# A recurrent scan on one core: the DMA queue in written order, stores one place later, solver pieces behind the state update, evictions on ScalarE, new pools

## The chip, the cores and the metric

The kernel runs on one core of a Trainium2 chip. A core has five engines that run their own instruction streams side by side: TensorE (PE, matrix multiplication; its weight loads are listed as PEld), VectorE (DVE), ScalarE (ACT), GpSimd (POOL) and SyncE (SP), whose queue issues the DMA transfers of this kernel. The metric is the device time of one execution in microseconds (us).

## The reference

One layer of a diffusion backbone on 128 context tokens and 1024 latent tokens of width 1024: a gated feed-forward, a mixer and a second gated feed-forward, each with a residual and a layer norm. The mixer projects its input once, and then runs an RWKV-7 branch and a pooling branch, gates both by channel, adds them and projects again. All of it is float32. Cut to the part that the change touches:

```
def _rwkv7_step(S, inp):                  # one token, both directions, 16 heads of 64
    r, w, k, v, kk, a = inp
    sa = jnp.einsum('dbhvk,dbhk->dbhv', S, kk)
    S = S * w[..., None, :] - sa[..., :, None] * (kk * a)[..., None, :] + v[..., :, None] * k[..., None, :]
    return S, jnp.einsum('dbhvk,dbhk->dbhv', S, r)
...
    s_final, y = lax.scan(_rwkv7_step, s0.astype(f32), xs)
    y = _from_scan(y)                     # forward plus reversed backward
    mu = jnp.mean(y, -1, keepdims=True)
    var = jnp.mean(jnp.square(y - mu), -1, keepdims=True)
    y = ((y - mu) * lax.rsqrt(var + GN_EPS)).reshape(b, t, D_A) * p['lnx_g'] + p['lnx_b']
    bonus = jnp.sum(r_h * k_h * p['r_k'], -1, keepdims=True) * v_h
    y = (y + bonus.reshape(b, t, D_A)) * g
    y_a = y.astype(h.dtype) @ p['w_o_rwkv']
    ...                                   # pooling branch: windows of 2, 4, 8, 16 tokens, w_pool, pool_scale
    y_b = u @ p['w_o_pool']
    gate_a = jax.nn.sigmoid(gate_logits[..., :D_MODEL])
    gate_b = jax.nn.sigmoid(gate_logits[..., D_MODEL:])
    return (gate_a * y_a + gate_b * y_b) @ p['w_out'], s_final
```

The latent scans start from given states (one for each direction); the context scans start from zero, and their last states are an output.

## The kernel before, in words

Tokens lie in NB = 3 blocks of 384. A float32 product is made of three matmuls: both operands are split into a high and a low part (`split`; for weights ACT makes `wh`, POOL or DVE `wl`), and high·high, high·low and low·high are added in PSUM. The stages follow each other: the first feed-forward, the mixer's input projection, a stage "m2", the scan (pools "s1" and "gn"), and then the rest of the mixer and the second feed-forward ("stage e" here).

The scan takes tokens in chunks of 64, both directions (d = 0, 1) at once, eight heads at a time: 18 chunks for each half of the heads, 36 steps. One step, `main(s)`, does the following. `xy` (L1042) multiplies the chunk's operands `ak` by the states `Sc`, and L1048 adds the part of the tokens before; the result is copied to `Xs`, d = 0 by ACT and d = 1 by DVE (L1052). `us` (L1058) multiplies `Xs` by the inverse `W` of a triangular matrix; it goes to `vu`, again by ACT and by DVE (L1062, L1064). `sp` (L1071) multiplies `vu` by the transposed keys `KBT`, and DVE adds it to the states and decays them (L1072, L1073). L1077 makes the output, ACT copies it to `yt` (L1081), and every second step stores it.

Between these parts lie three slots. Slot 0 stands behind the `Xs` copies, slot 1 behind `vu`, slot 2 behind the output. `slot_work(s, k)` puts into a slot a piece of a solver and one piece of each group norm under way, `fill(k)` some matmuls of `filler`. Slot 0 also has `pre(s+3)` (loads of `ak`, L998) and `pre_lm` (L1011 on PE, L1013 on DVE: the masked products `LM` for the next step); slot 2 is preceded by `load` (v of a unit of two steps, L985), `pre_kb` (transposes of keys, L1019) and `pre_lm`.

- `filler` is the gate and pooling branch: 900 matmuls of 128x384 outputs. `Halves` brings its weights in halves of 512 columns (load L139, ACT split L148, POOL split L149). `proj(n)` makes a gate from `hg` (the stored mixer input of blocks 1 and 2, loaded at L897), the four pool gemms (`pw`) take a pooled input `uf` (L923) each, and `back(n)` multiplies a gate by its branch (`gt`, L918) and stores it (`gab`, L919). AHEAD = 60 of them run before step 0. The others are spread over the slots in the ratio SPREAD = 6 : 9 : 10.
- `solve(i)` inverts the triangular 32x32 blocks of two units (four steps). It is a generator; `slot_work` takes a piece in each slot over four steps. It loads `Gq` and `Gt` (L758, eight DMAs), POOL transposes the half of d = 1 (L762), 31 pairs on DVE (L766, L768) work out both inverses, four pairs a slot, the result goes to memory and comes back in other layouts (`Wb`, `Dx`, `Nt`), and matmuls `ph` join the blocks to 64x64 inverses. Solvers 0 and 1 begin in m2, the other seven run in the scan.
- `group_norm(hb, tt)` is a generator in nine pieces for 128 tokens: loads and sums of `y`, the variance on DVE (L1122, L1123), a power on POOL (L1124), a product (L1125), four transposes on PE (L1132), scaling on ACT, the bonus on POOL (L1138) and the store `yn` (L1139). `drive` moves each running one by a piece; behind the last step a loop drives what is left, three pieces a round.

In the scan the order on PE, DVE, ACT and POOL is the order in which the code is written; the DMA queue of SP, and all engines outside of the scan, are ordered by a scheduler.

Of the kernel before, what the change touches and what calls it, by code (L numbers as in the profile page):

```python
# [2 lines left out]

# [17 lines left out]
AHEAD = 60  # L21
SPREAD = (6, 9, 10)
PWGAP = 4
# [37 lines left out]
def tile_step(ctx: ExitStack, tc: tile.TileContext, I: dict, O: dict):  # L61
# [68 lines left out]
    class Halves:  # L130
# [11 lines left out]
        def get(self, i, look=2):  # L142
            while len(self.got) < min(len(self.units), i + 1 + look):
                self.fetch(len(self.got) + 1)
                r = self.raws[len(self.got)]
                h = self.pool.tile([P, self.HW], F32R, name="wh", tag="wh", bufs=4)
                l = self.pool.tile([P, self.HW], F32R, name="wl", tag="wl", bufs=4)
                A.copy(h, r)  # L148
                G.tensor_tensor(l, r, h.bitcast(F32), ALU.subtract)  # L149
# [446 lines left out]
    with pool("mp", 4, psum=True) as psum, pool("ma", 2, psum=True) as paux, \  # L596
# [6 lines left out]
        with pool("m1") as pl:  # L603
# [11 lines left out]
            for p in range(NP):  # L615
# [26 lines left out]
                for b in range(NB):  # L642
# [79 lines left out]
                    S.dma_start(nd_d[1][p // 4][b][:, p % 4].rearrange("s c e t -> s (c e) t"), Qs[96:128, :, :, 0:32].rearrange("s c e t -> s (c e) t"))  # L722
# [24 lines left out]
        def solve(i):  # L747
            def t4(nm, tag_):
                return sv.tile([P, 32, 32], F32, name=nm, tag=tag_)
            Gq, Gt = t4("Gq", "gq"), t4("Gt", "pr")  # L750
            for k in range(2):
                u = 2 * i + k
                for d in range(2):
                    c0 = chunk0(u, d)
                    cb, cc, hb = c0 // 6, c0 % 6, u // 9
                    for hf in range(2):
                        p0 = d * 64 + hf * 32 + k * 16
                        S.dma_start((Gt if d else Gq)[p0:p0 + 16], qd_d[d][hb][cb][hf][:, cc:cc + 2].rearrange("a c e s t -> a (c e) (s t)"))  # L758
            Wd = t4("Wd", "wd")
            S.dma_start(Wd, I["id32"])  # L760
            yield
            G.tensor_copy(Gq[64:128], Gt[64:128].rearrange("p s t -> p t s"))  # L762
            pr = t4("pr", "pr")
            for k in range(31):
                o = pr[:, 0:k + 1, k + 1:32]
                V.tensor_tensor(o, Wd[:, 0:k + 1, k].unsqueeze(2).broadcast_to([P, k + 1, 31 - k]),  # L766
                                Gq[:, k, k + 1:32].unsqueeze(1).broadcast_to([P, k + 1, 31 - k]), ALU.mult)
                V.tensor_tensor(Wd[:, 0:k + 1, k + 1:32], Wd[:, 0:k + 1, k + 1:32], o, ALU.subtract)  # L768
                if k % 4 == 3:
                    yield  # L770
            ed = dram.tile([2, 2, 32, 32, 32], F32, name="ed", tag="ed", bufs=2)
            S.dma_start(ed.rearrange("d b n i t -> (d b n) i t"), Wd)
            yield
            W = Wb[i % 2]
            DT = Dx = t4("Dx", "dx")
            Mt = Nt = t4("Nt", "nt")
            for b in range(2):
                S.dma_start(W[32 * b:32 * b + 32, :, 32 * b:32 * b + 32], ed[0, b].rearrange("n i t -> i n t"))
                S.dma_start(Dx[64 + 32 * b:96 + 32 * b], ed[1, b].rearrange("n i t -> i n t"))
            for k in range(2):  # L780
                u = 2 * i + k
                for d in range(2):
                    c0 = chunk0(u, d)
                    S.dma_start(Nt[96 * d:96 * d + 32, k * 16:k * 16 + 16].rearrange("s (a n) t -> s a (n t)", a=4),
                                nd_d[d][u // 9][c0 // 6][:, :, c0 % 6:c0 % 6 + 2].rearrange("s a c e t -> s a (c e t)"))
            yield
            V.transpose(DT[0:32], W[0:32, :, 0:32])
            for b in range(2):
                r = slice(64 + 32 * b, 96 + 32 * b)
                V.transpose(W[r, :, 32 * b:32 * b + 32], Dx[r])  # L790
            yield

            def ph(jobs, k):
# [6 lines left out]
            for k in range(2):  # L800
                ks = slice(16 * k, 16 * k + 16)
                pm = ph(lambda n: ((slice(32, 64), Nt[0:32, n, :], DT[0:32, n, :]), (slice(64, 96), Nt[96:128, n, :], Dx[96:128, n, :])), k)
                A.copy(Mt[32:64, ks], pm[32:64])
                A.copy(Mt[64:96, ks], pm[64:96])
                yield
                pm = ph(lambda n: ((slice(0, 32), Mt[32:64, n, :], W[32:64, n, 32:64]), (slice(96, 128), Mt[64:96, n, :], W[64:96, n, 0:32])), k)
                A.mul(W[0:32, ks, 32:64], pm[0:32], -1.0)
                A.mul(W[96:128, ks, 0:32], pm[96:128], -1.0)
                yield

        CHAIN, TAILS, PPS = 11, 4, [paux, "aux"]
# [4 lines left out]
        for t in vus[0] + vus[1]:  # L816
            G.memset(t, 0.0)
        with pool("m2") as pl:
            sol0, sol1 = solve(0), solve(1)
            for _ in range(CHAIN + TAILS):  # L820
                next(sol0)
            for _ in range(CHAIN):
                next(sol1)
# [58 lines left out]

    def filler(psG):
# [7 lines left out]
        for b in range(NB):  # L891
            sl = slice(b * BN, (b + 1) * BN)
            hh = hs[0]
            if b:
                hh = [hpA.tile([P, KT, BN], F32R, name="hg", tag="hb") for k in range(2)]
                for k in range(2):
                    S.dma_start(hh[k].bitcast(F32), h2_d[b][k])  # L897
# [6 lines left out]
            def proj(n):  # L904
                ps = psG.tile([P, 512], F32, name="pm", tag="mm")
                for hf in range(2):
                    w = nextw(1 if n == 0 and hf else 2)
# [5 lines left out]
            def back(b, u2, gts, n):  # L913
# [5 lines left out]
                S.dma_start(gab_d[n][b][:, 1, :], gt)  # L919
# [8 lines left out]
            first = proj(0)  # L928
# [18 lines left out]
            for n in range(1, 8):  # L947
# [7 lines left out]
    with pool("s1") as pl, pool("gn") as gn, pool("spa", 2, psum=True) as psA, pool("spx", 1, psum=True) as psX, \  # L955
# [22 lines left out]
        def load(u):  # L978
            hb, q, cs = steps[2 * u]
            c = ctxs[u]  # L980
            for d in range(2):
                c0 = cs[d] // 2 * 2
                vh = slice(64, 128) if d == 0 else slice(0, 64)
                r0 = (c0 % 6) * 64
                S.dma_start(vus[d][u % 2][vh].rearrange("p k h v -> p k (h v)"),  # L985
                            vt_d[c0 // 6][r0:r0 + 128, 512 * hb:512 * hb + 512].rearrange("(k t) c -> t k c", k=2))
            c["W"] = Wb[u // 2 % 2][:, u % 2 * 16:u % 2 * 16 + 16].rearrange("p (a k e) t -> p a k e t", a=4, k=2)

        def pre(s):
            u = s // 2  # L990
            if s % 2 == 0:
                ctxs[u] = {"ak": {}, "LM": {}, "KBT": {}}
            hb, q, cs = steps[s]
            c = ctxs[u]
            c["ak"][s] = []
            for d in range(2):
                ak = pl.tile([P, 4, 256], F32, name=f"ak{d}", tag=f"ak{d}", bufs=3)
                S.dma_start(ak, ak_d[d][cs[d] // 6][cs[d] % 6, :, 4 * hb:4 * hb + 4])  # L998
                c["ak"][s].append(ak)
            c["LM"][s], c["KBT"][s] = {}, {}  # L1000

        def pre_lm(s, d):
            c = ctxs[s // 2]
            ak = c["ak"][s][d]
# [10 lines left out]
        def pre_kb(s, d):  # L1015
            c = ctxs[s // 2]
            pt = psM.tile([P, 4, P], F32, name="pt", tag="m")
            for i in range(4):
                PE.transpose(pt[:, i, :], c["ak"][s][d][:, i, 128:256], ident)  # L1019
# [3 lines left out]
        def main(s):  # L1023
# [6 lines left out]
            ak = c["ak"].pop(s)  # L1030
# [19 lines left out]
            for d in range(2):  # L1050
                x0, x1 = XR[d]
                (V.tensor_copy if d else A.copy)(eh(Xs[x0:x1]), xy[x0:x1, :, d])  # L1052
# [6 lines left out]
            for d in range(2):  # L1059
                x0, x1 = XR[d]  # L1060
                if d:
                    V.tensor_scalar(vu[d][x0:x1], us[x0:x1], -1.0, None, ALU.mult)  # L1062
                else:
                    A.mul(vu[d][x0:x1], us[x0:x1], -1.0)  # L1064
# [331 lines left out]
```

## Time and profile before

| | |
|---|---|
| median of three runs | 3551.59 us (3547.95 to 3558.2) |
| profiled execution, its own time | 3556.99 us |
| its span | 3555.2 us |
| mean granted TensorE clock | 0.943 |
| PE busy | 3263.3 us, 92% of the span, 25742 matmuls |
| DVE, ACT, POOL busy | 2053.9, 1104.4, 1315.4 us |
| scan, first step's first matmul to the last | 1707 to 2430 us |
| stage m2 | 1526 to 1652 us |

The profile is one execution. A row of a group names line, engine, operation, output and inputs with shapes and count, then busy time in us, the mean of one in ns, and the engine's idle time before them with what ended most of it. A row of the timeline gives start, length, engine and line, and in brackets the idle time before. The granted clock is a share of TensorE's full speed. The span does not hold 1.8 us of the execution's own time.

### The profile page before, as it was taken

The page shows a single profiled execution, that of the slowest core. Times are in us where ns is not written, and L with a number is a line of the kernel's source. Part 1 is how long each engine was busy: PE and PEld are TensorE (multiplying, and loading weights), DVE is VectorE, ACT ScalarE, POOL GpSimd, SP SyncE. Part 2 cuts the span into 40 slices and gives each one's busy share as a digit, 9 for nine tenths or more (in the row PEclk, how much of TensorE's full clock was granted, in tenths as well). Part 3 has the DMA queues.
Part 4 walks back from the last instruction along what each step waited for, and adds up shares of the span by engine and source line. Part 5 has one row for each costly group of instructions (what it writes and reads, how often), then busy time and mean ns, then how long its engine had stood idle before and what let it go on. Part 6 is the DMA issues. An engine that isn't in the chain of part 4 may idle for free.

```text
span 3555.2 us, 62714 instructions
## 1 busy us (share of the span) xinstructions
PE 3263.3 (92%) x25742; PEld 3094.7 (87%) x25742; DVE 2053.9 (58%) x3381; ACT 1104.4 (31%) x1898; POOL 1315.4 (37%) x1035
## 2 busy tenths in 40 slices
PE   7999999999999999787888777995999999999997
PEld 7999999998988877586777676885999999999996
DVE  6888532357467787855566676644576233222466
ACT  4111111125444444422333333333345111111133
POOL 5111111136466676643222343136774111111144
PEclk9999999999999999798898888997999999999998
DMA  6344211124645455465355555645652111111133
GB/s 232 127 144 133 75 48 37 54 89 143 217 146 160 155 160 155 144 199 169 117 151 188 148 155 174 170 123 172 223 177 66 40 45 37 48 48 36 48 124 108
DMA packets 309694, 442.74 MB, mean 125 GB/s; under 512 B 115360, under 2 KB 211104, under 8 KB 307872
## 3 DMA queue, kind: packets, MB, share of 16 engines
q1 hardware_dynamic: 309408, 438.74, 39.0%
q8 instruction: 202, 3.31, 0.4%
q14 instruction: 84, 0.69, 0.1%
HBM read 316.01 MB, written 101.25 MB: 117 GB/s over the span
## 4 chain that ended last, share of the span: by engine, by line
PE 58%; DVE 17%; DMA 8%; issue 7%; POOL 6%; ACT 3%; SPq 1%; DVEq 0%; POOLq 0%; ACTq 0%
PE pg L158 8%; PE pg L159 8%; PE pg L157 8%; PE po L158 5%; PE po L157 5%; PE po L159 4%; PE pm L158 2%; PE pm L157 2%; PE pm L159 2%; DVE Wd L768 2%; DVE pr L766 2%; DMA fm<-in_w_mod 2%; DVE wl L126 2%; PE xy L1042 2%; DVE fm L402 2%
## 5 line engine op out<-in xcount | busy, mean ns | idle before, releaser
L124 ACT CAST wh<-wr 128x1024 fp32r<-128x1024 f32 x270 | 280.3, 1048 | 818.2 <-PE po L158 432.9
L126 POOL TENSOR_TENSOR wl<-wr,wh 128x1024 fp32r<-128x1024 f32 x117 | 290.1, 2480 | 509.8 <-ACT wh L124 485.6
L294 POOL TENSOR_TENSOR gl<-sg,gh 128x384 fp32r<-128x384 f32 x132 | 159.0, 1205 | 780.6 <-ACT gh L293 780.5
L126 DVE TENSOR_TENSOR wl<-wr,wh 128x1024 fp32r<-128x1024 f32 x153 | 224.6, 1472 | 242.7 <-ACT wh L124 241.5
L157 PE MATMUL po<-gh,wh 128*128 128x384 f32 x1056 | 357.0, 338 | 7.4 <-ACT gh L293 4.3
L158 PE MATMUL pg<-h1l,wh 128*128 128x384 f32 x1056 | 356.6, 338 | 5.7 <-POOL h1l L166 5.7
L158 PE MATMUL po<-gl,wh 128*128 128x384 f32 x1056 | 357.7, 339 | 2.0 <-POOL gl L294 2.0
L157 PE MATMUL pg<-h1h,wh 128*128 128x384 f32 x1056 | 357.6, 339 | 0.0
L159 PE MATMUL po<-gh,wl 128*128 128x384 f32 x1056 | 355.8, 337 | 0.0
L159 PE MATMUL pg<-h1h,wl 128*128 128x384 f32 x1056 | 355.6, 337 | 0.0
L157 PE MATMUL pg<-h3h,wh 128*128 128x384 f32 x1056 | 353.7, 336 | 0.0
L159 PE MATMUL pg<-h3h,wl 128*128 128x384 f32 x1056 | 353.4, 335 | 0.0
L158 PE MATMUL pg<-h3l,wh 128*128 128x384 f32 x1056 | 353.2, 335 | 0.0
L291 DVE TENSOR_TENSOR sg<-sg,pg 128x384 f32<-128x384 f32 x132 | 74.2, 562 | 459.9 <-PE pg L159 453.9
L157 PE MATMUL pm<-h2h,wh 128*128 128x384 f32 x936 | 326.1, 348 | 3.7 <-ACT pads L441 3.7
L159 PE MATMUL pm<-h2h,wl 128*128 128x384 f32 x936 | 326.1, 348 | 0.0
L158 PE MATMUL pm<-h2l,wh 128*128 128x384 f32 x936 | 325.8, 348 | 0.0
L311 DVE SCALAR_TENSOR_TENSOR ac<-po,modh,ac 128x384 f32<-128x384 f32 (+1 forms) x352 | 173.0, 515 | 96.5 <-PE po L159 96.5
L149 POOL TENSOR_TENSOR wl<-wr,wh 128x512 fp32r<-128x512 f32 x75 | 96.5, 1292 | 321.9 <-ACT wh L148 264.2
L402 DVE SCALAR_TENSOR_TENSOR fm<-fm 128x512 f32<-128x512 f32 x224 | 182.3, 814 | 52.0 <-DMA fm<-in_w_mod 49.0
L157 PEld LDWEIGHTS po<-gh,wh 128*128 128x128 f32 x1056 | 199.1, 189 | 10.5 <-ACT gh L293 4.9
L158 PEld LDWEIGHTS pg<-h1l,wh 128*128 128x128 f32 x1056 | 200.5, 190 | 8.2 <-POOL h1l L166 7.7
(286 smaller groups left out, 7556.8 us busy)
## 6 DMA issues: line engine op xcount, KB each, us to landing
wr<-in_ffn_in SPq DMA_DIRECT2D x120, 512.0 KB
ak<-ak SPq DMA_DIRECT2D x48, 768.0 KB
ak<-ak SPq DMA_DIRECT2D x72, 512.0 KB
wr<-in_ffn_out SPq DMA_DIRECT2D x60, 512.0 KB
fm<-in_w_mod SPq DMA_DIRECT2D x112, 256.0 KB
wr<-in_w_mix SPq DMA_DIRECT2D x39, 512.0 KB
sh<-pads SPq DMA_DIRECT2D x108, 130.0 KB
wr<-in_w_mix SPq DMA_DIRECT2D x48, 256.0 KB
```

The source lines that it names most:

```text
L124: A.copy(h[:, :w], r[:, :w])
L126: e.tensor_tensor(l[:, :w], r[:, :w], h[:, :w].bitcast(F32), ALU.subtract)
L149: G.tensor_tensor(l, r, h.bitcast(F32), ALU.subtract)
L157: PE.matmul(ps, wh, xh, start=first and k == 0, stop=False)
L158: PE.matmul(ps, wh, xl, start=False, stop=False)
L159: PE.matmul(ps, wl, xh, start=False, stop=last and k == n - 1)
L291: lastv[0] = V.tensor_tensor(sg, sg, pu[:, :BN], ALU.mult)
L294: G.tensor_tensor(gs[j, b][1][:, sl], sg, gs[j, b][0][:, sl].bitcast(F32), ALU.subtract)
L311: lastv[0] = V.scalar_tensor_tensor(accs[b][:, n, s0:s1], po[:, s0:s1], modh[:, gate_i // 4, n, g:g + 1], accs[b][:, n, s0:s1], ALU.mult, ...
L402: V.scalar_tensor_tensor(jk, w, 1.0, silc[:, s, hf * 512:hf * 512 + 512], ALU.mult, ALU.mult, accum_out=part[:, kt, s, hf:hf + 1])
L766: V.tensor_tensor(o, Wd[:, 0:k + 1, k].unsqueeze(2).broadcast_to([P, k + 1, 31 - k]), Gq[:, k, k + 1:32].unsqueeze(1).broadcast_to([P, k + ...
L768: V.tensor_tensor(Wd[:, 0:k + 1, k + 1:32], Wd[:, 0:k + 1, k + 1:32], o, ALU.subtract)
```

## The change

- The DMA queue of SP joins the engines whose order in the scan is the written one.
- Stores of `y`, `yn` and `gab` in the scan are put on a list (`later`) and issued at the start of the next slot (`flush`).
- `solve` becomes a class with numbered pieces. Its pairs stand 2 in slot 0, 1 in slot 1 and 5 in slot 2, which lies behind the state update. The half of d = 1 is stored transposed already, by exchanging the operands of the matmul that makes it, so that the POOL copy goes. The parts that bring the inverse back take other places.
- The copies to `Xs` and `vu` of d = 1 move from DVE to ACT.
- A new pool `akp` holds `ak`; the loads of steps 0 to 2 and v of units 0 and 1 stand in m2, ahead of its gate work.
- AHEAD goes. 120 gate matmuls (TAILF) are kept for the time behind the last step: eight behind each drive, two drives a round in place of three. 780 are spread over the steps in place of 840.
- PWGAP is 10 in place of 4, and the matmuls between the pool gemms come from `proj(0)` and `proj(1)`. The `hg` loads move behind `back(6)` and `back(7)`, ahead of their first use, in four halves.
- `Halves.get` fetches one half ahead in place of two.
- A group norm has two more empty calls, one behind the power and one behind the bonus load's.

```diff
-AHEAD = 60
+TAILF = 120
-PWGAP = 4
+PWGAP = 10
...
-            self.fetch(len(self.got) + 2)
+            self.fetch(len(self.got) + 1)
...
+                                x, y = (al, be) if d else (be, al)
+                                pqs[b] = PE.matmul(pq[e][d * 64:d * 64 + 64, cc, :], ak[es, cc, x:x + 64], ak[es, cc, y:y + 64], start=True, stop=True)
...
+            def at(self, n):
+                if n == 0:
+                    self.loads()
+                elif n == 1:
+                    self.init()
+                elif n < 12:
+                    self.pairs((2, 1, 5)[n % 3])
+                elif n == 12:
+                    self.out()
+                elif n == 14:
+                    self.back()
+                elif n == 16:
+                    self.t0()
+                elif n == 17:
+                    self.t1(0)
+                elif n == 18:
+                    self.ph1(0)
+                elif n == 19:
+                    self.ph2(0)
+                elif n == 20:
+                    self.t1(1)
+                    self.ph1(1)
+                elif n == 21:
+                    self.ph2(1)
...
+            for s_, cs_ in enumerate(((0, 1), (1, 0), (2, 17))):
+                load_ak(s_, cs_, 0)
+            load_v(0, 0, (0, 1))
+            load_v(1, 0, (2, 17))
             for n in range(EARLY):
...
+    def later(out, in_):
+        lates.append((out, in_))
+
+    def flush():
+        while lates:
+            S.dma_start(*lates.pop(0))
...
-                for k in range(2):
-                    S.dma_start(hh[k].bitcast(F32), h2_d[b][k])
...
-                S.dma_start(gab_d[n][b][:, 1, :], gt)
+                later(gab_d[n][b][:, 1, :], gt)
...
-            first = proj(0)
+            if b:
+                for ks in (slice(0, 4), slice(4, 8)):
+                    for k in range(2):
+                        S.dma_start(hh[k][:, ks].bitcast(F32), h2_d[b][k][:, ks])
+            first = chain(proj(0), proj(1))
...
-                (V.tensor_copy if d else A.copy)(eh(Xs[x0:x1]), xy[x0:x1, :, d])
+                A.copy(eh(Xs[x0:x1]), xy[x0:x1, :, d])
...
-                if d:
-                    V.tensor_scalar(vu[d][x0:x1], us[x0:x1], -1.0, None, ALU.mult)
-                else:
-                    A.mul(vu[d][x0:x1], us[x0:x1], -1.0)
+                A.mul(vu[d][x0:x1], us[x0:x1], -1.0)
...
             G.tensor_tensor(vr, vr, half, ALU.pow)
+            yield
             G.tensor_tensor(y0, y0, vr.unsqueeze(2).broadcast_to([P, 8, 64]), ALU.mult)
...
             S.dma_start(bb, bon_d[hb][tt // 3][:, :, sl])
             yield
+            yield
...
-        quota = [3 * (12 + 8 * 36) - AHEAD, sum(SPREAD) * n]
+        quota = [3 * (12 + 8 * 36) - TAILF, sum(SPREAD) * n]
...
         def slot_work(s, k):
+            flush()
             for i in range(1, 9):
-                at = 3 * (s - 4 * i + 8) + k
...
+                n = 3 * (s - 4 * i + 8) + k
+                if 0 <= n < 24 and (i > 1 or n > 12):
+                    sols[i].at(n)
...
-        with tc.manual_schedule(engines={PE.engine, V.engine, A.engine, G.engine}):
+        with tc.manual_schedule(engines={PE.engine, V.engine, A.engine, G.engine, S.engine}):
...
-            for _ in range(AHEAD):
-                next(fl, None)
...
-                for _ in range(3):
+                for _ in range(2):
+                    flush()
                     drive(gns)
+                    for _ in range(8):
+                        next(fl, None)
```

The places where instructions move. First SP at the way into the scan, before: `Sc` are the states, `ak` the operands of steps 0 to 2, `gab` the gate stores of m2, `uf` and `wr` what `filler` loads, `bb` the bonus of a group norm.

```order
L971 DMA Sc_14682<-in_state 128x256
L830 DMA gab_1_117<-ga 128x384
L998 DMA ak_14689<-ak_0_80 128x1024
L998 DMA ak_14691<-ak_0_83 128x1024
L998 DMA ak_14695<-ak_0_80 128x1024
L998 DMA ak_14697<-ak_0_83 128x1024
L998 DMA ak_14699<-ak_0_80 128x1024
L998 DMA ak_14701<-ak_2_85 128x1024
L923 DMA uf<-u_191 128x384
L830 DMA gab_0_116<-ga 128x384
L923 DMA uf<-u_192 128x384
L139 DMA wr<-in_w_pool 128x512
```

The loads of `ak` stand behind all but the last of the gate stores. Afterwards the same queue has them ahead of the first gate store, with `v` (`vu`) behind them:

```order
L797 DMA Nt<-nd_0_2_181 32x4x128
L867 DMA ak_13845<-ak_0_80 128x1024
L867 DMA ak_13847<-ak_0_83 128x1024
L867 DMA ak_13849<-ak_0_80 128x1024
L867 DMA ak_13851<-ak_0_83 128x1024
L867 DMA ak_13853<-ak_0_80 128x1024
L867 DMA ak_13855<-ak_2_85 128x1024
L875 DMA vu_0_13526<-vt_86 64x2x512
L875 DMA vu_0_13528<-vt_86 64x2x512
L875 DMA vu_1_13527<-vt_86 64x2x512
L875 DMA vu_1_13529<-vt_88 64x2x512
L894 DMA gab_2_97<-ga 128x384
```

And this is what SP has afterwards where step 0 begins, behind the last gate store:

```order
L894 DMA gab_0_116<-ga 128x384
L867 DMA ak_14788<-ak_0_80 128x1024
L867 DMA ak_14790<-ak_2_85 128x1024
L765 DMA Gq<-qd_0_1_162 16x1x1024 x2
L765 DMA Gq<-qd_0_1_168 16x1x1024 x2
L765 DMA Gq<-qd_0_1_162 16x1x1024 x2
L765 DMA Gq<-qd_0_1_168 16x1x1024 x2
L994 DMA uf<-u_191 128x384
L994 DMA uf<-u_192 128x384
L140 DMA wr<-in_w_pool 128x512
L140 DMA wr<-in_w_mix 128x512 x4
```

The first weights of `filler` (`wr`) stand behind the operands of step 3 and the eight loads of a solver. On DVE, one step of the scan before, from the `Xs` copy to the state update; the pairs' shapes shrink and grow with their number:

```order
L1052 COPY Xs<-xy 64x2x4x64
L1013 TENSOR_TENSOR LM_15172<-pa,sc 128x4x128 x2
L766 TENSOR_TENSOR pr<-Wd,Gq 128x5x27
...
L768 TENSOR_TENSOR Wd<-Wd,pr 128x8x24
L1062 TENSOR_SCALAR vu_0_13528<-us 64x512
L766 TENSOR_TENSOR pr<-Wd,Gq 128x9x23
...
L768 TENSOR_TENSOR Wd<-Wd,pr 128x12x20
L1072 TENSOR_TENSOR Sc_14679<-Sc_14679,sp 128x256
L1073 TENSOR_TENSOR Sc_14679<-Sc_14679,PCst 128x256
```

Four pairs stand ahead of `vu` and four ahead of the update. Afterwards, in a step of the same kind, from one slot 2 to the next update (L776 and L778 are the pair, L1136 and L1137 the update):

```order
L776 TENSOR_TENSOR pr<-Wd,Gq 128x17x15
...
L778 TENSOR_TENSOR Wd<-Wd,pr 128x21x11
L1080 TENSOR_TENSOR LM_15565<-pa,sc 128x4x128 x2
L776 TENSOR_TENSOR pr<-Wd,Gq 128x22x10
...
L778 TENSOR_TENSOR Wd<-Wd,pr 128x23x9
L1178 TENSOR_REDUCE gmu<-y 128x8
L1179 TENSOR_SCALAR gmu<-gmu 128x8
L989 TENSOR_TENSOR gt<-gt,pb 128x384
L776 TENSOR_TENSOR pr<-Wd,Gq 128x24x8
L778 TENSOR_TENSOR Wd<-Wd,pr 128x24x8
L1136 TENSOR_TENSOR Sc_14683<-Sc_14683,sp 128x256
L1137 TENSOR_TENSOR Sc_14683<-Sc_14683,PCst 128x256
```

Both copies are gone from DVE, five pairs stand in slot 2, two in slot 0 and one ahead of the update.

More of the change, by code (lines that the diff above doesn't have):

```diff
@@ L2 @@
 from contextlib import ExitStack
+from itertools import chain
 import concourse.bass as bass
@@ L745, in tile_step, with __init__, t4 @@
             G.memset(t, 0.0)
-        def solve(i):
-            def t4(nm, tag_):
+        class Solve:
+            def __init__(self, i):
+                self.i, self.k = i, 0
+            def t4(self, nm, tag_):
                 return sv.tile([P, 32, 32], F32, name=nm, tag=tag_)
-            Gq, Gt = t4("Gq", "gq"), t4("Gt", "pr")
-            for k in range(2):
[L752 to L788, printed above, removed]
@@ new lines, in loads @@
+            def loads(self):
+                self.Gq = self.t4("Gq", "gq")
+                for k in range(2):
+                    u = 2 * self.i + k
+                    for d in range(2):
+                        c0 = chunk0(u, d)
+                        cb, cc, hb = c0 // 6, c0 % 6, u // 9
+                        for hf in range(2):
+                            p0 = d * 64 + hf * 32 + k * 16
+                            S.dma_start(self.Gq[p0:p0 + 16], qd_d[d][hb][cb][hf][:, cc:cc + 2].rearrange("a c e s t -> a (c e) (s t)"))
@@ new lines, in out, with back @@
+            def out(self):
+                self.pairs(31)
+                self.ed = dram.tile([2, 2, 32, 32, 32], F32, name="ed", tag="ed", bufs=2)
+                S.dma_start(self.ed.rearrange("d b n i t -> (d b n) i t"), self.Wd)
+            def back(self):
+                W = self.W = Wb[self.i % 2]
+                self.D = self.t4("Dx", "dx")
+                self.N = self.t4("Nt", "nt")
+                for b in range(2):
+                    S.dma_start(W[32 * b:32 * b + 32, :, 32 * b:32 * b + 32], self.ed[0, b].rearrange("n i t -> i n t"))
+                    S.dma_start(self.D[64 + 32 * b:96 + 32 * b], self.ed[1, b].rearrange("n i t -> i n t"))
+                for k in range(2):
+                    u = 2 * self.i + k
+                    for d in range(2):
+                        c0 = chunk0(u, d)
+                        S.dma_start(self.N[64 * d:64 * d + 32, k * 16:k * 16 + 16].rearrange("s (a n) t -> s a (n t)", a=4),
+                                    nd_d[d][u // 9][c0 // 6][:, :, c0 % 6:c0 % 6 + 2].rearrange("s a c e t -> s a (c e t)"))
@@ L817, in tile_step, with load_ak, load_v @@
             G.memset(t, 0.0)
-        with pool("m2") as pl:
[L819 to L823, printed above, removed]
+        akp = svctx.enter_context(pool("akp"))
+        aks = {}
+        def load_ak(s, cs, hb):
+            aks[s] = []
+            for d in range(2):
+                t = akp.tile([P, 4, 256], F32, name=f"ak{d}", tag=f"ak{d}", bufs=3)
+                S.dma_start(t, ak_d[d][cs[d] // 6][cs[d] % 6, :, 4 * hb:4 * hb + 4])
+                aks[s].append(t)
+        def load_v(u, hb, cs):
+            for d in range(2):
+                c0 = cs[d] // 2 * 2
+                vh = slice(64, 128) if d == 0 else slice(0, 64)
+                r0 = (c0 % 6) * 64
+                S.dma_start(vus[d][u % 2][vh].rearrange("p k h v -> p k (h v)"),
+                            vt_d[c0 // 6][r0:r0 + 128, 512 * hb:512 * hb + 512].rearrange("(k t) c -> t k c", k=2))
+        with pool("m2") as pl:
+            sols = [Solve(i) for i in range(9)]
+            for k in range(22):
+                sols[0].at(k)
+            for k in range(13):
+                sols[1].at(k)
+            for s_, cs_ in enumerate(((0, 1), (1, 0), (2, 17))):
+                load_ak(s_, cs_, 0)
+            load_v(0, 0, (0, 1))
+            load_v(1, 0, (2, 17))
             for n in range(EARLY):
@@ L946, in filler @@
             yield from first
-            for n in range(1, 8):
+            yield from back(b, u2, gts, 0)
+            for n in range(2, 8):
                 yield from proj(n)
@@ L979, in load @@
             hb, q, cs = steps[2 * u]
[L980 to L987, printed above, removed]
+            if u > 1:
+                load_v(u, hb, cs)
         def pre(s):
@@ L1138, in group_norm @@
             G.tensor_tensor(yo, yo, bb, ALU.add)
-            S.dma_start(yn_d[hb][tt // 3][:, :, sl], yo)
+            later(yn_d[hb][tt // 3][:, :, sl], yo)
         def drive(gens):
```

76 lines of the change are left out of this document (42 added, 34 removed).

## The prediction, made before the changed kernel had run

> **What bounds the kernel now.** I read the page's 40 slices first: TensorE (PE) is at 9 everywhere except before, in and after the scan. So I cut the span into windows there. Columns: length, then busy time of PE, weight load, VectorE (DVE), ScalarE (ACT), GpSimd (POOL), granted clock.
>
> ```profile
> 1526.00:1652.00 126.00, 116.26 (x875) 113.97 (x870) 80.70 (x138) 25.56 (x42) 57.08 (x44) 0.95 0.55 168
> 1652.00:1707.00 55.00, 27.26 (x121) 21.83 (x120) 7.57 (x9) 13.26 (x25) 16.50 (x15) 0.63 0.58 178
> 1707.00:2430.00 723.00, 610.89 (x10085) 549.12 (x10085) 456.67 (x892) 247.46 (x465) 213.62 (x167) 0.88 0.53 157
> 2281.00:2356.00 75.00, 75.00 (x1436) 67.70 (x1436) 36.93 (x65) 29.54 (x53) 14.84 (x12) 1.00 0.62 174
> 2430.00:2465.00 35.00, 9.02 (x43) 7.03 (x41) 11.30 (x24) 12.22 (x27) 26.24 (x19) 0.61 0.50 148
> ```
>
> In order: stage m2, the way into the scan, the scan, five scan steps inside it, the tail. The five steps run from one L1042 to another, rows of the timeline:
>
> ```profile
> 2281.20 0.55 PE L1042 MATMUL xy<-Sc,ak 64*128 64x64 f32 x6
> 2355.87 1.33 PE L1042 MATMUL xy<-Sc,ak 64*128 64x64 f32 x20
> ```
>
> They are 74.67/5 = 14.93 us a step with PE never idle, clock 1.00. Thirty-six would take 537.6; the scan takes 723. The 185.4 between are idle PE, 723 - 610.89 = 112.1, and the rest, 73.3, matmuls at a lower clock. Next, what PE waits for in the scan (us in total, times, longest), and the costly groups there:
>
> ```profile
> PE pt L1132 <- POOL y L1125: 53.5, 14, 5.5
> PE pt L1019 <- DVE Sc L1072: 28.0, 12, 3.7
> PE xy L1042 <- ACT yt L1081: 9.6, 2, 6.2
> PE us L1058 <- DVE Xs L1052: 3.3, 3, 1.9
> PE sp L1071 <- DVE vu L1062: 3.0, 5, 1.2
> ```
> ```profile
> L768 DVE TENSOR_TENSOR Wd<-Wd,pr 128x31 f32<-128x31 f32 (+15 forms) x217 | 95.2, 439 | 7.4
> L766 DVE TENSOR_TENSOR pr<-Wd,Gq 128x31 f32<-128x31 f32 (+15 forms) x217 | 90.8, 418 | 6.1
> L1013 DVE TENSOR_TENSOR LM<-pa,sc 128x512 f32<-128x512 f32 x138 | 88.9, 686 | 37.3 <-PE pa L1011 36.3
> L1073 DVE TENSOR_TENSOR Sc<-Sc,PCst 128x256 f32<-128x256 f32 x72 | 46.4, 644 | 2.5
> L1072 DVE TENSOR_TENSOR Sc<-Sc,sp 128x256 f32<-128x256 f32 x72 | 30.0, 417 | 59.0 <-PE sp L1071 58.1 <-POOL wl L149 0.6
> L1052 DVE COPY Xs<-xy 64x512 f32<-64x512 f32 x36 | 25.0, 695 | 149.3 <-ACT Xs L1052 149.1
> L1062 DVE TENSOR_SCALAR vu<-us 64x512 f32<-64x512 f32 x36 | 25.0, 695 | 14.0 <-ACT vu L1064 13.2
> L1064 ACT ACTIVATE vu<-us 64x512 f32<-64x512 f32 x36 | 21.2, 590 | 73.6 <-PE us L1058 73.5
> L149 POOL TENSOR_TENSOR wl<-wr,wh 128x512 fp32r<-128x512 f32 x68 | 87.8, 1294 | 286.4 <-ACT wh L148 263.2 <-DMA Nt<-nd 9.8 <-DMA ak<-ak 7.1
> ```
>
> Five waits make 97.4 of the 112.1. They are waits of a written order: group-norm transposes placed too close behind their POOL work, and state updates that stand behind eight solver operations on DVE. The scan is PE-bound wherever these are absent.
>
> **Way into the scan: -34.** PE stands still for the first ak, whose loads sit behind the gate stores on the DMA queue (SP; in timeline rows stand start, length, and in brackets the idle time before and what ended it):
>
> ```profile
> 1663.04 5.02 SPq L998 DMA_DIRECT2D ak<-ak  x6
> 1669.79 2.08 PE L1011 MATMUL pa<-ak 64*128 64x128 f32 x16 [17.77 <-DMA ak<-ak]
> 1670.98 0.33 SPq L139 DMA_DIRECT2D wr<-in_w_pool  x1
> 1680.57 0.69 PE L876 MATMUL pm<-h2h,wh 128*128 128x384 f32 x1 [3.28 <-ACT wh L148]
> 1707.01 0.55 PE L1042 MATMUL xy<-Sc,ak 64*128 64x64 f32 x6
> L758 SPq DMA_DIRECT2D Gq<-qd x36: 606/667/973, 1537.2 to 2229.4; - x36
> ```
>
> Afterwards ak and v are issued in m2, ahead of its gate work, so they have landed, and no 60 gate matmuls stand between. What stays ahead of step 0 is three L1011/L1019 groups: 1669.79 to about 1678 at half clock, some 5 to 6 at full. The first step starts at 1652 + 6 instead of 1707: -49. But the first gate weight now stands behind that step's SP work: two ak (5.02/6 each), eight solver loads at 0.667, uf, about 7.9 us of queue, and then 1680.57 - 1670.98 = 9.6 to its first matmul: 17.5, less about 4.5 of PE work in step 0 that doesn't need it: +13, and 2 for a cold clock behind that. Ends: 0 (SP ran ahead) and 20.
>
> **Scan: -117.5.**
> - Waits. Stores move one place later, so SP no longer stops at a store whose data is not made; this takes from PE's own table nothing directly. Two more empty calls in group norm put a slot between POOL's L1125 and the transposes: -53.5. DVE runs its pairs 2, 1 and 5 a slot, the five behind the state update, and gives both evictions to ACT: -28.0 and -6.3. The yt waits I take as gone too, -9.6: one of the two (3.39) ends 2.3 us behind the issue of the hg loads (rows below), which have moved. If they stay, 9.6 and 6.3 of clock come back. Together 97.4, or 87%; 11.8 of waits of the pool gemms (L876, L878) and small ones I leave as they are. ACT takes 72 x 0.59 = 42 us more, 290 of 605: covered by the matmuls that follow each eviction in the slot.
> - Clock. How matmuls slow after a wait, from the timeline:
>
> ```profile
> 1735.41 0.66 PE L1019 MATMUL pt<-cst,ak 128*128 128x128 f32 x4 [2.73 <-DVE Sc L1072]
> 1874.22 3.43 PE L1042 MATMUL xy<-Sc,ak 64*128 64x64 f32 x32 [3.39 <-ACT yt L1081]
> 2341.17 2.00 PE L1042 MATMUL xy<-Sc,ak 64*128 64x64 f32 x32
> ```
>
>   After 3.39 us of idle the 32 matmuls take 3.43 instead of 2.00; after 2.73 nothing is lost. I give back 87% of 73.3: -63.7. Ends: 0 and 73.3. The Trainium skill, "TensorE: Matmul & The Clock Gate", Part 1, says that the clock halves after an idle window of about 3.4 us which runs free of the program; the two rows agree. By that rule the Sc waits (2.3 us on average) cost no clock and the long ones all of it, so all 73.3 would return, 10 us more than I take.
> - Gate matmuls. 780 instead of 840 are spread over the steps. One occupies PE from its start to the next one's, 0.17:
>
> ```profile
> 2429.44 0.34 PE L880 MATMUL pb<-u,wl 128*128 128x384 f32 x1
> 2429.61 0.33 PE L876 MATMUL pb<-u,wh 128*128 128x384 f32 x1
> ```
>
>   60 x 0.174 = -10.4, or 0.29 a step.
> - hg loads. Now they lead their first use by 21 us and nobody waits:
>
> ```profile
> 1871.90 0.96 SPq L897 DMA_DIRECT2D hg<-h  x2
> 1893.13 0.69 PE L876 MATMUL pm<-hg,wh 128*128 128x384 f32 x1
> DMA packets 4330, 11.37 MB, mean 284 GB/s; under 512 B 483, under 2 KB 1088, under 8 KB 4071
> ```
>
>   They move directly ahead of that use. The first half (two of 768 KB) at 284 GB/s is 5.5 us, plus some 3.5 (an estimate: the issues, two of 0.5, and what is in flight before them): 9 at each of two blocks, +18. Ends: 0, if SP runs that far ahead of PE, and 2 x 15, if all 3 MB must land (11 us) behind a full queue.
> - DVE. A pair is 0.439 + 0.418 = 0.857, and 217 pairs are seven inverses of 31. A step with an inverse (four to each, 28 in all) has 8 pairs (6.9), four L1013 (2.6), two updates (76.4/36 = 2.1), and its share of the other groups ((456.67 - 401.3 of those listed)/36 = 1.5): 13.1, against 14.93 - 0.29 = 14.64 of PE. Five of the eight pairs now stand between one update and the next slot; DVE must be through with all before the next sp is made. That leaves 1.5 us for every wait of DVE on PE. I add 1 us in each of the 28 steps: +28 (ends 0 and 86, worked out under B). The L762 copy that goes from POOL and the transposed store that replaces it lie off this path: 0.
> - Late weights. Fetching one half weight ahead instead of two, in a queue that is written: +8, one us at each of eight inverses' loads. Ends 0 and rival C.
>
> -97.4 - 63.7 - 10.4 + 18 + 28 + 8 = -117.5; the scan becomes 605, or 16.8 a step.
>
> **Tail: +17.** Columns as above; PE, SP and ACT/POOL rows:
>
> ```profile
> 2446.29 1.11 PE L1132 MATMUL pt<-cst,y 128*128 128x128 f32 x4 [10.96 <-POOL y L1125]
> 2464.55 0.69 PE L157 MATMUL pm<-yh,wh 128*128 128x384 f32 x1 [2.04 <-ACT yh L165]
> 2409.98 0.34 SPq L121 DMA_DIRECT2D wr<-in_g_up  x1
> 2415.30 2.34 POOL L126 TENSOR_TENSOR wl<-wr,wh 128x1024 fp32r<-128x1024 f32 x1 [6.08 <-ACT wh L124]
> ```
>
> Today 34.5 us, POOL 26.24 of it busy, PE waiting. 120 gate matmuls now lie here (21 us of PE, hidden), but their ten half weights add 10 x 1.29 to POOL, and group norm takes two more calls. POOL: 22.8 of group norm + 12.9 = 35.7, +3 for the last chain. Stage e's first weight was issued 54 us ahead of its need; now it stands behind the last stores: 2415.30 + 2.34 - 2409.98 = 7.7 until ready, and its own gemm, 6; 3 of this overlap: 49 to 50. With the cold weight pipeline +17. Ends: -5 (gate matmuls hide it all) and +30.
>
> **Stage m2: 0.** The two solvers' parts take other places, PE is idle for 9.7 us there; ends -10 and +10.
>
> **Sum.** -34 - 117.5 + 17 = -134.5 on the profiled execution's 3557.0 (span 3555.2 and 1.8 around it): 3422.5. That execution is 5.4 above the median of the runs, 3551.59; I forecast 3417.
>
> **Rivals.**
> - A, the cover holds: no new wait at hg, DVE, late weights or the first weight: 54 + 13 less, 3350. For it: five steps in the trace that run so. Against: DVE is busy for only 36.93 of 75 in those, there being no inverse left.
> - B, DVE becomes the bound of inverse steps. The state update varies today:
>
> ```profile
> L1073 DVE TENSOR_TENSOR Sc<-Sc,PCst x72: 424/425/2199, 1716.5 to 2429.8; 128x256 f32<-128x256 f32 x72
> ```
>
>   72 x 0.425 would be 30.6, it takes 46.4: something holds it. If half of POOL's 213.62/36 = 5.9 a step falls on DVE, and it waits 58.1/36 = 1.6 for sp as now, a step takes 13.1 + 3.0 + 1.6 = 17.7, 3.1 over PE's: 28 x 3.1 = 86 instead of 28, 3475. The Trainium skill, "SBUF — State Buffer", section "SBUF: two separate sides", says that a DVE operation with two SBUF inputs and a GpSimd operation that reads SBUF share one port pair, and the later one blocks wholly; the range up to 2199 agrees. By that rule B is what a denser scan would bring.
> - D, the group-norm wait returns, since the power on POOL waits for a DVE sum that now stands behind five pairs: 53.5 and its clock (53.5/97.4 x 63.7 = 35) stay: 3505. Against: two free calls are more than the 5.5 that is its longest.
> - C, the other side: half weights come late. SP in a written order stops where one load waits, and everything behind it, the next weight too, waits with it; its lead is one half, 12 matmuls or 0.55 step, 8 us, against 17.5 from the working above when solver loads stand ahead. 780/12 = 65 half weights; from 134/65 = 2.1 us lost at each the gain is gone. At 3.5 each: 3417 - 8 + 228 = 3637. For it: SP's written place behind solver loads. Against: only one step in four has them.
>
> **How the numbers follow.** Forecast 0.54 (its own range 3385 to 3450), A 0.15, B 0.16, D 0.06, C 0.09. The point is the forecast's, 3417. The range goes from 3345 (A just inside) to 3515 (B and D inside); outside stay C and the half of A below, under 0.2. Faster by over 0.3%, about what a measurement of this kernel tells from no change: all but C, 0.89; C's near edge gives 0.02 within it, and 0.09 slower.
>
> **What would show it.** The first L1042 at 1652 to 1662 and a wait for wh some 13 us long behind it; no transposes waiting for POOL in the scan; DVE's update at once behind sp; clock in the scan at 0.96 or more; a wait of about 9 at each first hg matmul; scan length 605; tail near 52. Wrong it is if PE's waits in the scan name weight splits (C), the update (B), or if the scan's clock stays under 0.92.

## The result, and the profile after

The changed kernel takes 3471.12 us (median of four runs, 3456.81 to 3476.58) against 3551.97 us before: 0.9765 of the time, 95% interval 0.9731 to 0.9799. That is faster, inside the range, and 54 us above the point of the forecast. The profiled execution has a span of 3474.5 us, 80.7 less than before.

The same windows as before the change (length; busy PE, PEld, DVE, ACT, POOL; clock): m2, the way into the scan, the scan, and the tail up to the first matmul on `yh`. The scan ends, as in the window before the change, with the last gate matmul of the last step's slot.

```profile
1530.00:1668.00 138.00, 119.39 (x873) 116.76 (x869) 79.02 (x138) 25.86 (x43) 54.33 (x39) 0.91 0.54 173
1668.00:1676.00 8.00, 6.90 (x67) 5.20 (x68) 3.53 (x6) 1.83 (x4) 0.00 (x0) 1.00 0.07 25
1676.00:2325.00 649.00, 569.71 (x10021) 512.10 (x10020) 407.76 (x816) 290.80 (x538) 203.53 (x164) 0.91 0.59 172
2325.00:2382.00 57.00, 34.78 (x165) 31.89 (x164) 16.63 (x28) 20.22 (x43) 37.65 (x30) 0.82 0.59 188
```

The end of m2 comes 16 us later (1668 for 1652). The way in is 8 long for 55. The scan is 649 for 723, and the tail 57 for 34.5. With +1.8 in the rest: 16 - 47 - 74 + 22.5 + 1.8 = -80.7. TensorE's waits inside the scan are other ones than before (us in total, times, longest):

```profile
PE us L1125 <- ACT Xs L1119: 15.3, 4, 7.9
PE pm L940 <- ACT wh L149: 12.9, 1, 12.9
PE pm L940 <- DMA hg<-h: 10.6, 2, 7.9
PE xy L1109 <- ACT yt L1145: 9.0, 3, 6.8
PE sp L1135 <- ACT vu L1128: 8.9, 2, 5.6
PE pt L1086 <- DVE Sc L1136: 5.4, 4, 4.2
```

The transposes' wait for POOL, 53.5 before, is not in the list at all, and that for Sc fell from 28.0 to 5.4. Three rows name evictions on ScalarE. What ScalarE itself waited for in the scan, and SP:

```profile
ACT wh L149 <- DMA wr<-in_w_mix: 60.2, 10, 14.0
ACT wh L149 <- DMA wr<-in_w_op: 28.8, 8, 5.9
ACT wh L149 <- DMA wr<-in_w_pool: 12.7, 2, 11.4
SPq L867 <- PE xy L1109: 103.5, 20, 19.8
SPq L954 <- DVE gt L989: 33.0, 8, 9.0
```

Before the change ScalarE's casts of half weights (x68) had 0.2 us of idle time ahead of them in all; now it is 101.7. SP stands for 103.5 us at the `ak` loads, whose buffer the running step still reads (L867 was L998, where it waited 57.6). It also stands at stores that were put off by one place (L954, in `flush`), 33.0 us for the gate product alone. One place shows the chain, SP first, then ScalarE, then TensorE:

```profile
1769.78 4.90 SPq L791 DMA_DIRECT2D Wb<-ed  x1
1774.72 1.22 SPq L792 DMA_DIRECT2D Dx<-ed  x1
1775.99 2.53 SPq L797 DMA_DIRECT2D Nt<-nd  x4
1778.62 0.53 SPq L140 DMA_DIRECT2D wr<-in_w_mix  x1
1781.60 0.62 ACT L149 CAST wh<-wr 128x512 fp32r<-128x512 f32 x1 [5.67 <-DMA wr<-in_w_mix]
1782.13 1.20 ACT L1128 ACTIVATE vu<-us 64x512 f32<-64x512 f32 x2
1782.77 1.97 PE L1135 MATMUL sp<-vu,KBT 128*64 128x64 f32 x32 [5.58 <-ACT vu L1128]
```

A half weight is issued behind a solver's loads, its cast waits for the landing, the `vu` eviction is written behind that cast, and TensorE waits for `vu`. The weight itself is for later gate matmuls.

### The profile page after: what moved, and what is told of

It is laid out like the page before. It is cut to its first block, busy times and chain, and to the rows that moved or that the text cites. A ratio compares the mean times of both kernels' runs of the same rounds, so it can differ in the third digit from the quotient of the medians.

```text
span 3474.5 us, 62657 instructions
## 1 busy us (share of the span) xinstructions
PE 3236.0 (93%) x25742; PEld 3072.7 (88%) x25742; DVE 1999.5 (58%) x3309; ACT 1149.4 (33%) x1970; POOL 1311.7 (38%) x1026
## 4 chain that ended last, share of the span: by engine, by line
PE 60%; DVE 14%; DMA 10%; issue 5%; POOL 5%; SPq 3%; ACT 3%; DVEq 0%; POOLq 0%; ACTq 0%
PE pg L159 8%; PE pg L160 8%; PE pg L158 8%; PE po L158 5%; PE po L159 5%; PE po L160 5%; PE pm L158 2%; PE pm L160 2%; PE pm L159 2%; PE pa L1078 2%; DVE wl L127 2%; PE xy L1109 2%; DMA fm<-in_w_mod 1%; DVE pr L776 1%; DVE Wd L778 1%
```

## The experiments

Each ratio is against the kernel before, from runs on the same chip. Theory C is the prediction's rival C: a written DMA queue makes something late. Unless said otherwise, rows of waits are from the scan. Idle time and slow matmuls are worked out as in the prediction: idle is the window less PE's busy time, slow is what is left above 36 undisturbed steps of 14.64 us, 527 (an estimate).

**e1: half weights fetched two ahead.** Base: the changed kernel.

```diff
-            self.fetch(len(self.got) + 1)
+            self.fetch(len(self.got) + 2)
```

> The changed kernel, but half weights are fetched two ahead again. Theory C (half weights come late: the cast of one on ScalarE waits for its landing, and the evictions to Xs, vu and yt wait behind it): ScalarE's waits for landings of half weights in the scan, 101.7 us in the changed kernel, fall to below 40, TensorE's waits for ScalarE behind Xs, vu and yt (33 us) to below 15, and the time falls by 15 to 35 us. Rival (VectorE or the clock alone holds the scan back): no change, within 8 us.

0.9750 (0.9732 to 0.9767), 3460.87 us: not told apart from the changed kernel: in time this is the rival, within 8 us. ScalarE's waits for half weights did fall, from 101.7 to 13.9. But others came up: hg 20.4 for 10.6, vu 18.9 for 8.9, Sc 21.4 for 5.4. The longest behind `vu`, with SP ahead of ScalarE and TensorE:

```profile
1992.04 0.60 SPq L954 DMA_DIRECT2D yn<-yo  x1
1999.96 1.50 ACT L1202 ACTIVATE yo<-pt,par 128x128 f32<-128x128 f32 x4 [12.95 <-DMA yn<-yo]
2001.98 1.98 PE L1135 MATMUL sp<-vu,KBT 128*64 128x64 f32 x32 [10.96 <-ACT vu L1128]
```

The same place, the same eviction held, but by a group-norm store that has not left its buffer. So the half weights are only one of the things that come late.

**e2: the DMA queue left to the scheduler.** Base: the changed kernel.

```diff
-        with tc.manual_schedule(engines={PE.engine, V.engine, A.engine, G.engine, S.engine}):
+        with tc.manual_schedule(engines={PE.engine, V.engine, A.engine, G.engine}):
```

> The changed kernel, but the DMA queue of SyncE is ordered by the scheduler again, everything else as changed. Theory C (the written order of the queue makes half weights late): ScalarE waits less for half weights, scan shorter by 10 to 30 us. Rival (the written order is what removed the waits of the scan before): the scan gets longer by 30 us or more.

0.9633 (0.9599 to 0.9668), 3422.85 us: the written queue costs (0.9765 - 0.9633) x 3551 = 47 us. The scan window and TensorE's longest waits in it:

```profile
1675.00:2272.00 597.00, 550.19 (x10021) 494.34 (x10019) 405.74 (x815) 290.52 (x538) 202.39 (x164) 0.96 0.63 184
```
```profile
PE pt L1086 <- DVE Sc L1136: 21.4, 7, 4.4
PE ph L811 <- issue: 9.3, 5, 2.9
PE pw L940 <- DVE gt L989: 9.1, 1, 9.1
```

597 for 649, more than the 10 to 30 expected; the waits behind Xs and yt are gone or below 1 us, vu is at 1.8, hg doesn't appear, and the first half weight costs 1.4 instead of 12.9. Idle falls by 32.5 (79.3 to 46.8), slow matmuls by 19.5 (42.7 to 23.2). Behind the last step a transpose (L1198) waits 3.8 more for Sc.

**e3: a solver's DMAs behind the gate matmuls of their slot.** Base: the changed kernel. Pieces 0, 1 and 14 of `at` are called at the end of `fill`:

```diff
+                    if n in (0, 1, 14):
+                        behind.append((sols[i], n))
+                    else:
+                        sols[i].at(n)
```

> The changed kernel, but the DMAs of a solver (the loads of Gq, of Wd, and those that bring the inverse back) are issued behind the gate matmuls of the same slot and so behind the half weights fetched there. Theory C: they no longer stand ahead of the half weights of their slot; TensorE's 33 us of waits behind Xs, vu and yt fall to below 15, time 15 to 30 us less. Rival (something else delays the half weights, the operands ak whose buffer is not free): no change, within 8 us.

0.9786 (0.9762 to 0.9811), 3471.68 us: no gain. The waits behind Xs, vu and yt fell from 33.2 to 16.4, nearly as far as theory C says, but TensorE now waited for the state update:

```profile
PE pt L1086 <- DVE Sc L1136: 21.5, 6, 5.0
```

That the solver's later DMAs made it so is not shown: VectorE's waits for landings ahead of pairs are 57.0 for 48.1, but e1 and e2, with these DMAs in their place, have 21.4 behind Sc too.

**e4: hg loads early.** Base: the changed kernel, the four loads ahead of `back(6)` and `back(7)`.

> The changed kernel, but the hg loads stand ahead of the last two gate products of the block before, as they did before the change, still in four pieces. Theory: the two waits for hg (13.2 us) and their cold clock go, 10 to 20 us less. Rival: 3 MB sent earlier delay the stores of yt or the half weights, which cost the same again: no change.

0.9765 (0.9742 to 0.9788), 3466.33 us: no change, the rival. The wait for hg has gone from the list, and one behind yt has come:

```profile
1912.98 3.68 PE L1108 MATMUL xy<-Sc,ak 64*128 64x64 f32 x32 [15.25 <-ACT yt L1144]
```

**e5: pairs one slot later.** Base: e2. The first pair of an inverse starts late, and the trace names a landing, a row of e2:

```profile
1758.48 0.19 DVE L776 TENSOR_TENSOR pr<-Wd,Gq 128x31 f32<-128x31 f32 x1 [5.66 <-DMA Wb<-ed]
```
```diff
-                elif n < 12:
-                    self.pairs((2, 1, 5)[n % 3])
+                elif 2 < n < 12:
+                    self.pairs((3, 2, 5)[n % 3])
```

> The changed kernel with the DMA queue left to the scheduler (3422.85), and the solver's pairs start one slot later, 3, 2 and 5 a slot in place of 2, 1 and 5. Theory D (the remaining state-update waits, 25 us in 8 places about one inverse apart, come from the first pair of an inverse, which waits on VectorE for its operands' landing, 5.7 us in the row at 1758.5, and everything behind it is late): the waits fall below 8 us and the time by 15 to 30 us, to about 3400. Rival B (VectorE has too much work in such a step): one more pair a step ahead of the update makes the waits longer, time the same or up to 20 us more.

0.9613 (0.9593 to 0.9632), 3411.02 us: 7 us by the ratios, and the two intervals overlap. VectorE's waits for landings ahead of pairs fell from 42.0 (three rows of e2's groups) to 1.8, so theory D names a real wait; but TensorE's waits for Sc did not go:

```profile
PE pt L1086 <- DVE Sc L1136: 19.2, 12, 3.8
```

They are twelve shorter ones for seven. One pair more stands in slot 0 and one more in slot 1, both ahead of the update; this fits rival B, at 1.6 us a wait.

**e6: ak and v loads among the gate matmuls of m2.** Base: e2.

```diff
             for n in range(EARLY):
+                if 2 <= n < 5:
+                    load_ak(n - 2, ((0, 1), (1, 0), (2, 17))[n - 2], 0)
+                elif 5 <= n < 7:
+                    load_v(n - 5, 0, ((0, 1), (2, 17))[n - 5])
```

> The changed kernel with the DMA queue left to the scheduler, and the ak and v loads of the first steps stand one step each between the gate matmuls of m2, not all ahead of them. Theory (those loads, 7.6 us of queue behind 8 us of solver loads, hold up a gate store; both buffers of a gate are then full and TensorE waits 11.2 us): the wait falls to below 3 us, 8 to 15 us less, about 3412. Rival (the wait comes from the solver's loads and window sums, which the loads of ak only follow): the same wait, the time within 5 us.

0.9634 (0.9619 to 0.9648), 3419.61 us: no change, as the rival has it for the time; the wait itself went, as the theory has it. The waits of TensorE in m2, two rows of e2 and then two of e6:

```profile
PE pm L158 <- ACT ga L893: 11.2, 1, 11.2
PE ph L811 <- DVE Dx L801: 4.6, 1, 4.6
```
```profile
PE ph L811 <- DVE Dx L801: 10.5, 1, 10.5
PE pa L1078 <- ACT ga L893: 7.9, 1, 7.9
```

The wait that the loads had caused is gone, and two others took its place: the first inverse, which the 11.2 had covered, and the last gate's store.

**e7: the d = 1 copies back on VectorE.** Base: e2, L1119 and L1128 as before the change.

> The changed kernel with the DMA queue left to the scheduler, and the d = 1 copies to Xs and vu on VectorE as before the change. If the move to ScalarE is what freed the state update: VectorE has 1.4 us more a step, behind five pairs; TensorE's waits for Sc, Xs and vu rise from 27 to 50 us or more, 30 to 60 us slower, about 3470. Rival (the copies were cheap where they stood): within 10 us.

0.9663 (0.9645 to 0.9682), 3429.68 us: about 10 us slower by the ratios, and the intervals overlap: in time that is the rival. The waits did rise where the copies now stand:

```profile
PE us L1125 <- DVE Xs L1119: 30.3, 9, 8.6
PE sp L1138 <- DVE vu L1129: 9.7, 9, 2.2
```

With 7.2 of Sc that is 47 us of waits for 23 in e2, where Sc has 21.4 and vu has 1.8. Other waits shrank (for `gt` from 9.1 to nothing, at L811 from 9.3 to 2.8), so that all idle time grew by only 9 us (55.5 for 46.8).

**e8: the kernel before with a written DMA queue.** Base: the kernel before, the edit of e2 the other way round.

> The kernel before, with one edit: the DMA queue too is in the written order in the scan. It has its stores in their old places, so the queue stops at each y store until its data is made, and at hg and ak. If a written queue costs by itself: slower than before by 40 us or more, with ScalarE waiting for half weights. Rival (the cost needs the new places of the solver's loads): within 15 us of before.

1.0136 (1.0117 to 1.0154), 3595.63 us against 3548.93: 48 us slower by the ratio, with none of the other parts. ScalarE's waits for half weights rise from 0.2 to 34.3, and TensorE's waits behind VectorE's `Xs` copy from 3.3 to 54.1; what makes that copy late was not followed. The wait for POOL stays as it was:

```profile
PE us L1058 <- DVE Xs L1052: 54.1, 7, 11.1
PE pt L1132 <- POOL y L1125: 51.1, 14, 5.8
```

**e9: what was best together.** e5 with the loads of e6, and four buffers of their own for the gates in m2.

```diff
-                    ga = s0.tile([P, 8, 64], F32, name="ga", tag="Xs", bufs=2).rearrange("p h v -> p (h v)")[:, :BN]
+                    ga = pl.tile([P, BN], F32, name="ga", tag="ga", bufs=4)
```

> The DMA queue left to the scheduler, the solver's pairs one slot later (3411.02 by itself), the ak and v loads among the gate matmuls of m2, and four buffers of its own for a gate there in place of two. Theory (a gate waits for a store behind queue work of 8 to 17 us; four buffers are 17 us of TensorE work): the waits for gates in m2 and at its end go, 11 to 18 us less than with the pairs alone, about 3396. Rival (the wait for the first inverse in m2, 4.6 to 10.5 us, grows by what the gates gain): within 6 us of 3411.

0.9616 (0.9600 to 0.9633), 3412.94 us: as e5. Here m2 waits 7.0 for the first inverse, 6.0 for `LM`, 3.7 for a weight and 2.9 for a gate, and the first step starts at 1670.4 as in e6. The gates were not what held m2.

**e10: group norm in nine calls.** Base: e2, the two empty `yield`s taken out.

> The changed kernel with the DMA queue left to the scheduler (3422.85), and a group norm in nine calls as before, without the two empty ones. If these freed the transposes: their 53.5 us of waits for POOL and some 35 of cold clock come back in the scan, 60 to 90 us more, about 3495. Rival (the new order of VectorE's work, not the calls, freed them): within 15 us.

0.9727 (0.9708 to 0.9746), 3453.00 us: 33 us slower than e2. The wait is back:

```profile
PE pt L1196 <- POOL y L1189: 41.5, 13, 4.2
PE pt L1086 <- DVE Sc L1136: 8.7, 4, 3.8
```

The kind was right and the size was below the 60 to 90 expected: Sc fell from 21.4 to 8.7 at the same time, so that the idle time grew by 24.5 us net (71.3 for 46.8) and slow matmuls by 10.5.

**e11: four pairs in every slot.** Base: e2.

```diff
-                    self.pairs((2, 1, 5)[n % 3])
+                    self.pairs(4 if n < 10 else 0)
```

> The changed kernel with the DMA queue left to the scheduler, and the solver's pairs four in each slot, as before the change, in place of 2, 1 and 5. If their place behind the state update is what freed it: TensorE's waits for Sc rise from 25 us to 50 or more, 20 to 50 us more. Rival (with the copies gone from VectorE the place matters little): within 10 us.

0.9836 (0.9815 to 0.9857), 3492.66 us: 72 us slower than e2, more than expected.

```profile
PE pt L1086 <- DVE Sc L1136: 49.1, 13, 8.0
PE xy L1109 <- ACT yt L1145: 31.2, 5, 13.3
```

Sc came back as expected; the second row was not. `yt` has one buffer, and the trace shows ScalarE's copy to it held while SP issues the stores that empty it behind a solver's loads (SP, then ScalarE):

```profile
1996.49 1.64 SPq L954 DMA_DIRECT2D y<-yt  x2
2006.41 1.17 ACT L1145 COPY yt<-xy 64x512 f32<-64x512 f32 x2 [17.70 <-DMA gab<-gt]
```

From 1987.32 to 1993.86 SP had issued those loads (L792, L797). That it is these stores is argued from the one buffer; the named releaser is a store issued just behind them. So the 72 us are not shown to be the place of the pairs alone, and why the scheduler put the stores so late was not followed.

**e12: stores issued at once.** Base: the changed kernel with its written queue.

```diff
-        lates.append((out, in_))
+        S.dma_start(out, in_)
```

> The changed kernel with its written DMA queue, but the stores of y, yn and gab issued where their data is made, not one place later. If a store stops a written queue until its data is made: ScalarE's waits for half weights rise above 101.7 us and the time by 20 to 60 us. Rival (the queue is held by the ak loads and the solver's anyway): within 10 us of 3471.

0.9853 (0.9834 to 0.9872), 3499.73 us: 31 us slower than the changed kernel. ScalarE's waits for half weights rise from 101.7 to 132.5, as expected, and hg's row rises from 10.6 to 27.0:

```profile
PE pm L940 <- DMA hg<-h: 27.0, 2, 15.3
PE us L1125 <- ACT Xs L1119: 23.4, 7, 7.7
```

So the later stores earn 31 us of what a written queue costs.

## Why the prediction was right, and where it was not

- **Way into the scan, -34: right.** 47 us gained there, and behind it one wait of 12.9 for the first half weight where 13 was worked out, with a slow clock behind it:

```profile
1675.73 2.00 PE L1109 MATMUL xy<-Sc,ak 64*128 64x64 f32 x32
1692.85 0.69 PE L940 MATMUL pm<-h2h,wh 128*128 128x384 f32 x1 [12.95 <-ACT wh L149]
```

  The first step started at 1675.7 and not at 1652 to 1662, for what m2 had lost. The early loads of `ak` and the dropped 60 gate matmuls were not undone one at a time.
- **Stage m2, 0: too small, it was +16.** Twelve of this are in the stage (138 long for 126), four lie ahead of it. The step costed the moved loads at their new place at nothing and did not name what stands behind them on SP. It is the gate stores, rows of the changed kernel:

```profile
1554.49 4.89 SPq L867 DMA_DIRECT2D ak<-ak  x6
1559.47 2.66 SPq L875 DMA_DIRECT2D vu<-vt  x4
1563.04 2.00 SPq L894 DMA_DIRECT2D gab<-ga  x2
```
```profile
PE pm L158 <- ACT ga L893: 11.7, 1, 11.7
```

  e6 and e9 show that this wait can be taken away without gain, since the inverse and, in e6, the last gate's store or, in e9, `LM` are waited for next. The four us ahead of m2 are not explained.
- **Scan waits removed, -97.4: right in kind, and in size for POOL and most of the update.** The POOL row is gone, and Sc is at 5.4 for 28.0. The yt row, which was to go, is at 9.0 for 9.6, and Xs and vu are at 15.3 and 8.9; with the queue free (e2) yt and vu are at 0.8 and 1.8 and Xs is gone. Undone one at a time on e2: the pairs' place 72 (31.2 of idle behind `yt` is in it), the empty calls 33, the copies about 10.
- **New waits: the total right, the parts not.** The prediction left 14.7 of idle and added 13, 18, 28 and 8: 81.7. Measured idle is 649 - 569.71 = 79.3. But hg took 13.2 for 18 and DVE 5.4 for 28, while the waits behind Xs, vu and yt, to which late half weights lead in part (the chain above; e1, e3), took 33.2 where 8 stood for late weights. That the sum agrees is chance.
- **Clock, -63.7: the step that failed.** It returned 87% of 73.3 for the waits removed, and charged no cold clock for the 67 us of waits that the same sum added, except 2. At 36 x 14.64 = 527 for an undisturbed scan, 649 - 527 - 79.3 = 43 us were still lost to a lower clock, where 9.6 and 2 stood in the sum: +31. The row at 1692.85 above shows it behind a new wait: 0.69 us for a gate matmul that takes 0.34 elsewhere. With the queue free 19.5 of the 43 go together with 32.5 of idle. The old ratio would have given 73.3/112.1 x 67 = 44 for the new waits, and 9.6 + 44 = 54: 11 too much, but nearer than 12. The ratio is no constant: worked out the same way, slow time per us of idle was 0.65 before, 0.54 after and 0.34 in e1, with 86.7 us of idle. The scan's clock of 0.91 fell under the 0.92 that the prediction named as a sign against it.
- **Tail, +17: right in kind, 5.5 too small**, 22.5. POOL works 37.65 of the 57 where 35.7 was worked out. A half weight, issued only at 2367.67, costs TensorE 3.5, and stage e's first weight, issued at 2369.49, is ready at 2378.1.
- **Rival C, 0.09: its mechanism was there, at a third of its price.** It was held to be worth 2.1 us a half weight before it decides; the written queue cost 47/65 = 0.7 us each, counted with all else that it makes late (e2, and 48 in e8). It did not decide. The working for it held that SP no longer stops at stores whose data is not made; it does, 33.0 us at the gate stores alone (L954). B was not seen as a bound: the Sc row is at 5.4, and with the queue free at 21.4 (e2), under B's 86. D did not come, the wait for POOL is gone; A did not, since the new waits came. The forecast's 3417 is what the change gives without its first part (e2, 3422.85): by chance, since the sum holds other parts too.

Sum of the misses: m2 16, way in 2 (47 gained for 49), scan 29 (649 for 605 and 15 of the first weight), tail 5.5, the rest 1.8: 54.

## What to carry to other kernels

A new wait costs its idle time and the slow clock behind it: where waits removed are credited with clock, waits added must be charged with it too; the rate is a rough one (0.34 to 0.65 us for each us idle here). An in-order queue that is written by hand makes every entry wait for the slowest ahead of it: here that cost 47 us. Mending one late item (weights, hg, a solver's loads) only brought up the next (e1, e3, e4); compare the whole queue written and left to the scheduler before tuning single entries. When loads are moved ahead on a shared queue, list the stores behind them and count those stores' buffers.

## What the runs showed of the hardware

The state update's second operation (L1137, before L1073) reads two tiles of SBUF. Set against POOL's operations in time, its 72 cases fall into two kinds: before the change 50 beside no POOL operation took 424 to 428 ns, and 22 that overlapped one took 1142 ns on average; after it 29 took 424 to 427 and 43 took 937. First rows of e2 with POOL at work (DVE, then POOL), then with POOL idle:

```profile
1748.47 0.42 DVE L1136 TENSOR_TENSOR Sc<-Sc,sp 128x256 f32<-128x256 f32 x1 [1.57 <-PE sp L1135]
1748.93 1.23 DVE L1137 TENSOR_TENSOR Sc<-Sc,PCst 128x256 f32<-128x256 f32 x1
1748.61 1.27 POOL L150 TENSOR_TENSOR wl<-wr,wh 128x512 fp32r<-128x512 f32 x1
...
1768.40 0.42 DVE L1137 TENSOR_TENSOR Sc<-Sc,PCst 128x256 f32<-128x256 f32 x1
```

L1136, whose second operand lies in PSUM, took 0.42 in both. The Trainium skill, "SBUF — State Buffer", section "SBUF: two separate sides", has the rule that a DVE operation with two SBUF inputs and a GpSimd operation that reads SBUF exclude each other; the two kinds agree. More of the updates met POOL after the change (43 of 72 for 22), as rival B held, and yet TensorE's waits for Sc in the scan fell, from 28.0 to 5.4.
